# Latent attention: row maxima of two key pieces together, with a 32-row rotary part from the query's high part alone

## The chip, the cores and the metric

The kernel runs on one core of a Trainium2 chip. The metric is the device time of one execution in microseconds (us), as the median of several runs. The core's engines are called as the profile calls them: PE (matrix unit; its weight loads are listed apart as PEld), DVE (vector), ACT (scalar, activations), POOL (GpSimd) and SP (the queue from which most transfers are issued). PE multiplies a stationary operand (the weights, up to 128x128) with a moving one of up to 512 columns, and writes into PSUM, which has eight banks of 512 float32 columns on 128 partitions. A matmul whose operands use only 64 of the 128 partitions is put on half of PE's rows (a tile of 64 rows); in this kernel's timeline two such matmuls on different halves run side by side. The change uses tiles of 32 rows as well.

## The reference

Two layers over 1024 latent tokens and 256 context tokens of width 1024: the first is windowed attention, the second is multi-head latent attention (16 heads, 64 plain and 32 rotary dimensions for a query and a key, 64 for a value), then a final RMS norm. The change is in the second layer's attention:

```python
def attend(qn, qr, kn, kr, v):
    s = (jnp.einsum("bqhd,bkhd->bhqk", qn, kn)
         + jnp.einsum("bqhd,bkd->bhqk", qr, kr)).astype(F32) * scale
    p = jax.nn.softmax(s, axis=-1).astype(v.dtype)
    return jnp.einsum("bhqk,bkhd->bqhd", p, v)
```

The rotary keys `kr` are the same for all heads. All inputs are float32.

## The kernel before

Products are made in a fast float32 format of PE. Where more precision is wanted, an operand is split into a high and a low part of that format, and the product is made of several matmuls (high x high, low x high, high x low). `split` makes the two parts of an operand: a cast on ACT and a subtraction on DVE (or POOL).

The attention of the second layer is made in 16 units (`class UnitB`). A unit is a pair of heads and half of the latent queries (512). The two heads `e` of a pair lie on the two halves of the partitions (`HALF`), so that their matmuls run as a pair on PE's two 64-row halves. The 1280 keys are taken in ten chunks of 128 for the scores and three pieces of 512, 512 and 256 (`KEYB`) for the maxima. The operands of a unit are:

- `kt`, the plain part of the keys of the pair, high and low, and `KR`, the rotary part, repeated four times over the partitions, so that each 32 rows hold all of it; `KR[:, 0]` is the high part;
- `q`, the queries, in four slots: 0 and 1 are the plain part (high, low); in slot 2 the first 32 rows of each half hold the rotary high part and the other 32 rows the rotary low part; in slot 3 the first 32 rows of each half hold the rotary high part, and rows 32 to 35 the negated maxima, which `shift` writes there. `prep` loads them from DRAM, with one load for slots 0 and 1 and two per head for the rotary ones.

For each unit:

- **Maxima** (`top`, L1754 its matmuls, L1760 and L1762 its reductions). With queries as stationary operand and keys as moving one, a piece is two matmuls per head: slot 0 with the high plain keys (64 rows), and slot 2 with `KR[:, 0]` (64 rows: the query's high and low rotary parts with the key's high part). They add up in one bank per head. DVE then takes the maximum over the bank's columns. There are four blocks `b` of 128 queries and three pieces `i` of keys; the 256-wide pieces are taken two blocks together in one bank. `PIECES` is the list of ten, one for each score chunk. The banks come from a ring of three (`topb`: 0, 1, 2), which the fills share.
- **Shift** (`turn`, `shift`). The maxima of a unit are joined, turned by PE and written as four more rows of the query operand, so that the scores come out with the maximum subtracted.
- **Scores** (`score`, L1788). For each chunk `c` five matmuls per head, terms 0 to 4; the last has 36 rows, 32 rotary ones and four of the shift. `bank(c)` alternates between two pairs of banks (3 and 4, 5 and 6). When the fifth term is issued, `exp(c)` (L1798) follows on ACT, one activation over both banks, and POOL adds it up for the sum of the softmax (L1802, L1804).
- **PV** (`PV`, L1811). The exponentials of each chunk with the values, in 128x64 tiles, added up in bank 7 over all ten chunks. `fin` copies bank 7 out on ACT (L1815) and loads the gate. `fin2` makes the sum over partitions (L1822), `inv` the reciprocal, `gate` the product with the gate on POOL.
- **Fill**. Between units, `make_K` (each other unit) or `make_V` (each fourth unit) makes the keys of the next pair or the values of the next four heads with 128-row matmuls (L285 to L287).

Everything from the units on is issued in program order; each engine takes its own instructions in that order. The loop over units interleaves them by hand: the maxima of the next unit `nu` are made between the scores of the present unit `u`. In each chunk PE takes score terms 0 to 2, then one piece of the next unit's maxima, then score terms 3 and 4. After the ten chunks, `prep` of the unit after the next is issued, PV(0), the sums of the previous unit, PV(1) to PV(4), the turn of the next unit's maxima, PV(5) to PV(9), then a fill where there is one, then `fin`. The maxima of unit 0 are made ahead of the loop, with banks that are named there. So the loop makes the maxima of 15 units.

```python
u.score(c, 0, CUT)
if nu:
    nu.top(PIECES[c])
if c == 0 and ui > 1:
    units[ui - 2].gate()
u.score(c, CUT, 5)
```

Of the kernel before, what the change touches and what calls it, by code (L numbers as in the profile page):

```python
# [16 lines left out]
AX = mybir.AxisListType  # L17
# [18 lines left out]
class Ring:  # L36
# [6 lines left out]
    def next(self):  # L43
        b = self.bufs[self.i % len(self.bufs)]
        self.i += 1
        return b


def shp(ap, *dims):
    n = 1  # L50
    for d in dims:
        n *= d
    ap = ap[:, 0:n]
    if len(dims) == 1:
        return ap
    names = "abcdefg"[: len(dims)]
    kw = {c: d for c, d in zip(names[1:], dims[1:])}
    return ap.rearrange("p (" + " ".join(names) + ") -> p " + " ".join(names), **kw)
# [159 lines left out]
def kernel(ctx: ExitStack, tc: tile.TileContext, t, out, dbg=None):  # L218
    plan = Plan()
    nc = Recorder(tc.nc, plan)  # L220
# [4 lines left out]
    PB = ppool.tile([128, 8, 512], F32, name="PB")  # L225
# [16 lines left out]
    load = nc.sync.dma_start  # L242
    load2 = nc.scalar.dma_start

    def r_at(kb, *dims):
        n = int(np.prod(dims))
        return shp(R[:, int(kb * KB) : int(kb * KB) + n], *dims)
# [298 lines left out]
    for p in (1, 3):  # L546
        two = R[:, 16 * p * KB : 16 * (p + 2) * KB]
# [105 lines left out]
    class UnitA:  # L653
# [23 lines left out]
        def prep(self):  # L677
            ti, g = self.ti, self.g
            self.gt = shp(gr.next(), 2, 128)
            load(out=self.gt, in_=g0_d[2 * g : 2 * g + 2, :, ti * 128 : ti * 128 + 128].rearrange("c p n -> p c n"))  # L680
            self.mx, self.nm, self.den, self.esk = sm_ring(), sm_ring(), sm_ring(), sm_ring()
# [195 lines left out]
    def turn(p, b, bank):  # L877
        tbank[p, b] = ps = shp(PB[:, bank, :], 2, 256)
        for kk in range(2):
            for j in range(2):  # L880
                c0 = (2 * b + kk) * 128
                nc.tensor.transpose(ps[:, kk, j * 128 : j * 128 + 128], xn[p][0][:, j, c0 : c0 + 128], ident)
# [129 lines left out]
    for i in range(3, NG):  # L1012
        p, q = groups[i]
# [47 lines left out]
    for bi, gp, c in order:  # L1061
# [20 lines left out]
        r = proj_t(bi, gp, c)  # L1082
# [43 lines left out]
    for ui, u in enumerate(units):  # L1126
# [9 lines left out]
        nu = units[ui + 1] if ui + 1 < len(units) else None  # L1136
# [4 lines left out]
        for ci in range(u.m):  # L1141
# [3 lines left out]
            if ci == 0:  # L1145
# [6 lines left out]
                if ui in (24, 27, 30, 33, 36):  # L1152
                    i = ui // 3 - 8
# [3 lines left out]
            i = u.g * u.m + ci - 1  # L1157
# [338 lines left out]
    for k in range(8):  # L1496
        w0_cut1(k, nc.vector if k % 2 else nc.gpsimd)
        if k % 2:
            b = k // 2
# [4 lines left out]
    def turn_two():  # L1504
        if todo:
            p, b = todo.pop(0)
            for i in range(2):
                turn1(p, b + i, turns)
            return p, b
# [14 lines left out]
    two = turn_two()  # L1524
# [10 lines left out]
    two = turn_two()  # L1535
    for ti in range(NT):
# [6 lines left out]
        now, two = two, turn_two()  # L1543
# [11 lines left out]
        if 4 <= ti < 8:  # L1555
            i = ti - 4
# [32 lines left out]
    for n, i in enumerate((2, 3, 4, 5, 0, 1)):  # L1589
        ps = product(a12r[i], B21)  # L1590
        x = outs.next()
# [65 lines left out]
    KR = r_at(20, 2, TOK)  # L1657
# [4 lines left out]
    otr = Ring(F, [0, 2], 512)  # L1662
    glr = Ring(R, [30, 112, 150], 512)
    KEYB = ((0, 512), (512, 512), (1024, 256))
    PIECES = [[(0, 0)], [(0, 1)], [(1, 0)], [(1, 1)], [(0, 2), (1, 2)]]
    CUT = 3
    PIECES += [[(b + 2, i) for b, i in p] for p in PIECES]
    flat = krF.rearrange("p a b -> p (a b)")
    mxr = [flat[:, 128 * i : 128 * i + 128] for i in range(2)]
    mxpr = [shp(flat[:, 256 + 24 * i : 280 + 24 * i], 2, 4, 3) for i in range(2)]  # L1670
    ones = sm(64)
    nc.vector.memset(ones, 1.0)
    fillb = Banks(0, 1, 2)
    topb = Banks(0, 1, 2)
    psd = PB[:, 5, :]
    HALF = [slice(64 * e, 64 * e + 64) for e in range(2)]

# [16 lines left out]
    def make_V(quad):  # L1694
        for tp in range(NP):
            ps = fillb()
            for j in range(2):
                ti = 2 * tp + j
                for k in range(2):
                    mm3(  # L1700
                        ps[:, j * 256 : j * 256 + 256],
                        [ckvT[:, s, k, ti * 128 : ti * 128 + 128] for s in range(2)],
                        [ukV[:, s, k, quad * 256 : quad * 256 + 256] for s in range(2)],
                        k == 0, k == 1,
                    )
            nc.scalar.copy(Vq[:, 2 * tp : 2 * tp + 2], shp(ps, 2, 4, 64))
            yield

    def make_K(pair):
        kt = kTb[pair % 2]  # L1710
        for n0, n in KEYB:
            ps = fillb()
            for k in range(2):
                mm3(
                    ps[:, 0:n],
                    [ukK[:, s, k, pair * 128 : pair * 128 + 128] for s in range(2)],
                    [ckvT[:, s, k, n0 : n0 + n] for s in range(2)],
                    k == 0, k == 1,
                )
            split(kt[:, 0, n0 : n0 + n], kt[:, 1, n0 : n0 + n], ps[:, 0:n])  # L1720
            yield
# [3 lines left out]
    class UnitB:  # L1725
# [11 lines left out]
        def prep(self):  # L1737
            q = self.q.bitcast(F32)
            load(out=q[:, 0:2], in_=qn_d[self.pair, :, :, self.ts])
            for e in range(2):  # L1740
                r = 32 * ((2 * self.pair + e) % 4)
                src = qr_d[self.pair // 2, r : r + 32, :, self.ts]
                load(out=q[64 * e : 64 * e + 32, 2:4], in_=src[:, 0:1].to_broadcast([32, 2, 512]))
                load(out=q[64 * e + 32 : 64 * e + 64, 2], in_=src[:, 1])

        def top(self, piece, banks=None):

            banks = banks or (topb(), topb())
            n = KEYB[piece[0][1]][1]
            for j, (b, i) in enumerate(piece):  # L1750
                n0, o, bs = KEYB[i][0], 256 * j, slice(b * 128, b * 128 + 128)
                for s, k in ((0, self.kt), (2, KR)):
                    for bank, r in zip(banks, HALF):
                        nc.tensor.matmul(  # L1754
                            bank[:, o : o + n], self.q[r, s, bs], k[r, 0, n0 : n0 + n], start=s == 0, stop=s == 2
                        )
            b, i = piece[0]
            for e, bank in enumerate(banks):
                if len(piece) == 1:
                    nc.vector.reduce_max(self.mxp[:, e, b : b + 1, i], bank[:, 0:n], AX.X)  # L1760
                else:
                    nc.vector.reduce_max(self.mxp[:, e, b : b + 2, i], shp(bank, 2, 256), AX.X)  # L1762

        def turn(self, bank):
            nc.vector.reduce_max(shp(self.mx, 2, 64)[:, :, 32:36], self.mxp, AX.X, negate=True)
# [96 lines left out]
    def fetch_out(ti):  # L1862
        o = shp(ogl.next(), 8, 128)
        load(out=o.bitcast(F32), in_=og_d[:, :, ti * 128 : ti * 128 + 128].rearrange("c p n -> p c n"))
        x = xr1.next().bitcast(F32)
        load(out=x, in_=x1_d[256 + ti * 128 : 384 + ti * 128, :])
        return o, x

    def cut_out(f):
        o, x = f  # L1870
        og = shp(ogr1.next(), 2, 8, 128)
        for h in range(2):
            hs = slice(4 * h, 4 * h + 4)
            split(og[:, 0, hs], og[:, 1, hs], o[:, hs].bitcast(F32))
        return og, x
# [87 lines left out]
    fillb = Banks(6, 7)  # L1963
# [11 lines left out]
    fillb = Banks(0, 1, 2)  # L1975
    nc.scalar.activation(const[:, 1:2], const[:, 1:2], AF.Exp)
    wo_fill = wo_pieces()
    for ui, u in enumerate(units):
        pu = units[ui - 1] if ui else None
        nu = units[ui + 1] if ui + 1 < NU else None  # L1980
        nnu = units[ui + 2] if ui + 2 < NU else None
        for c in range(NT):
            if c == 5 and nu is None:
                pu.fin2(PB[:, 2, :])
                u.PV(0, 5)
                pu.inv(0)
                pu.gate(0, 256)
                first = fetch_out(0)
                pu.inv(1)
                pu.gate(256, 512)  # L1990
                got = fetch_out(1)
            u.score(c, 0, CUT)
            if nu:
                nu.top(PIECES[c])
            if c == 0 and ui > 1:
                units[ui - 2].gate()
            u.score(c, CUT, 5)
            if 0 < ui < 12 and c == 2 or ui == 6 and c == 7 or ui in (12, 13) and c in (2, 7):
                next(wo_fill, None)
            if nu is None and c == 0:  # L2000
                load(out=gx1, in_=gate_d[1, 0, :].partition_broadcast(128))
                load(out=fg, in_=t["final_g"].partition_broadcast(128))
        if nnu:
            nnu.prep()
        if nu is None:
            u.PV(5, NT)
        else:
            b = u.bank(NT - 2)
            u.PV(0, 1)
            u.exp(NT - 1)  # L2010
            if pu:
                pu.fin2(PB[:, b, :])
            u.PV(1, 5)
            nu.turn(PB[:, b + 1, :])
            nu.shift()
            if pu:
                pu.inv(0)
                pu.inv(1)
            u.PV(5, NT)
        if nu:  # L2020
            fillb.i = topb.i
            fill = make_K(u.pair + 1) if u.half == 0 and u.pair < 7 else iter(())
            if ui % 4 == 3:
                fill = make_V(ui // 4 + 1)
            for _ in fill:
                pass
        else:
            ready = cut_out(first)
        u.fin()
    u.fin2(psd)  # L2030
    for j in range(2):
        u.inv(j)
# [78 lines left out]
```

## Time and profile before

| what | before |
|---|---|
| median of 3 runs | 1489.13 us (1488.36 to 1490.11) |
| the profiled execution | 1488.73 us, its span 1486.9 us |
| mean granted clock of PE | 0.997 |
| busy: PE, DVE, ACT, POOL | 98%, 72%, 49%, 55% of the span |
| the 16 units of latent attention | from about 927 to 1393 us of the span |
| one scoring stage (ten chunks of one unit; units 0 to 14) | 16.5 to 16.8 us |
| one PV stage | 9.8 us, then a fill of 3.65 or 7.4 us, or none |

A line of a group reads: line of the kernel, engine, operation, what is written from what, shapes (partitions x elements), count, then busy time and the mean of one, then idle time ahead of it with what ended most of it. A timeline's row gives the start and length of a run of equal instructions in us, the engine, the line, the operation, the shape of the first one, and the count; in brackets stands the idle time ahead of it and what ended it. Matmuls overlap, so that the sum of their lengths is more than their busy time; the distance from start to start tells what one costs.

### The profile page before, as it was taken

What the parts mean: (1) busy time and instruction counts of PE and PEld (TensorE: products, weight loads), DVE (VectorE), ACT (ScalarE), POOL (GpSimd) and SP (SyncE); (2) the same over time, 40 slices, a digit from 0 to 9 for tenths busy, and PEclk for the clock granted to TensorE, in tenths of its full rate; (3) what the DMA queues carried; (4) which work ended last, traced back from release to release, by engine and by line L of the source; (5) the groups of instructions that cost most, each with busy time, mean ns of one, the idle gap of its engine ahead of it and who ended that gap; (6) DMA issues with size and microseconds to landing.
All of it is one profiled execution on the core that took longest, in us unless ns stands there. A gap on an engine that the chain in (4) does not pass through costs nothing.

```text
span 1486.9 us, 25072 instructions
## 1 busy us (share of the span) xinstructions
PE 1462.6 (98%) x9036; PEld 1188.3 (80%) x9036; DVE 1064.1 (72%) x2029; ACT 733.5 (49%) x1397; POOL 810.4 (55%) x735
## 2 busy tenths in 40 slices
PE   6999999999999999999999999999999999999998
PEld 4888888888888888888888888766777767876687
DVE  3787789738778888878988777666576466566764
ACT  4421222359888878876554432443454344444321
POOL 2563366346454444456300240798788788789371
PEclk9999999999999999999999999999999999999999
DMA  9545644673343333336444566011122212120442
GB/s 336 170 171 170 212 150 169 208 223 114 121 144 119 98 101 98 100 100 229 119 120 119 169 234 207 21 41 53 47 63 70 62 47 61 54 68 28 151 152 86
DMA packets 146964, 186.01 MB, mean 125 GB/s; under 512 B 12812, under 2 KB 100492, under 8 KB 146840
## 3 DMA queue, kind: packets, MB, share of 16 engines
q1 hardware_dynamic: 141864, 177.75, 37.7%
q10 hardware_dynamic: 4976, 6.66, 1.3%
q8 instruction: 71, 1.16, 0.3%
q14 instruction: 53, 0.43, 0.1%
HBM read 134.02 MB, written 46.15 MB: 121 GB/s over the span
## 4 chain that ended last, share of the span: by engine, by line
PE 49%; DVE 2%; issue 1%; DMA 0%; POOL 0%; ACT 0%; POOLq 0%; DVEq 0%; ACTq 0%
PE PB L1788 13%; PE PB L1811 9%; PE PB L285 7%; PE PB L287 7%; PE PB L286 7%; PE PB L1754 5%; PE PB L1822 1%; DVE arena_r L281 1%; DMA arena_r<-arena_f 0%; PE PB L1768 0%; DVE arena_f L1327 0%; DVE krF L1760 0%; DVE arena_f L1236 0%; DVE arena_f L1329 0%; DVE arena_f L1328 0%
## 5 line engine op out<-in xcount | busy, mean ns | idle before, releaser
L285 PE MATMUL PB<-arena_r 128*128 128x512 f32 (+2 forms) x1200 | 439.4, 366 | 1.3 <-DVE arena_f L1236 1.3
L286 PE MATMUL PB<-arena_r 128*128 128x512 f32 (+2 forms) x1200 | 433.7, 361 | 0.1
L287 PE MATMUL PB<-arena_r 128*128 128x512 f32 (+2 forms) x1200 | 433.3, 361 | 0.0
L1804 POOL TENSOR_TENSOR arena_f<-arena_f 128x1024 f32<-128x1024 f32 x120 | 285.9, 2382 | 8.2
L285 PEld LDWEIGHTS PB<-arena_r 128*128 128x128 f32 x1200 | 226.3, 189 | 45.7 <-issue 9.0
L287 PEld LDWEIGHTS PB<-arena_r 128*128 128x128 f32 x1200 | 226.3, 189 | 33.7
L286 PEld LDWEIGHTS PB<-arena_r 128*128 128x128 f32 x1200 | 226.5, 189 | 32.2 <-POOL arena_r L281 0.8
L1788 PE MATMUL PB<-arena_r 64*128 64x512 f32 (+1 forms) x1600 | 229.6, 395 | 0.0
L1798 ACT ACTIVATE arena_f<-PB 128x1024 f32<-128x1024 f32 x160 | 164.5, 1028 | 112.0 <-PE PB L1788 84.0
L1760 DVE TENSOR_REDUCE krF<-PB 128x1 f32<-128x512 f32 (+1 forms) x264 | 167.0, 678 | 65.7 <-PE PB L1754 65.6
L1788 PEld LDWEIGHTS PB<-arena_r 64*128 64x128 f32 (+1 forms) x1600 | 179.4, 185 | 14.7 <-issue 5.2
L704 DVE CUSTOM_DVE_ANT_0 arena_f<-PB,arena_f,small 128x256 f32<-128x256 f32 (+1 forms) x288 | 148.1, 525 | 51.9 <-PE PB L698 33.3
L280 ACT CAST arena_r<-PB 128x512 fp32r<-128x512 f32 (+2 forms) x207 | 115.3, 564 | 113.2 <-PE PB L287 73.3
L281 DVE TENSOR_TENSOR arena_r<-PB,arena_r 128x512 fp32r<-128x512 f32 (+2 forms) x207 | 134.3, 661 | 34.7 <-ACT arena_r L280 34.1
L1811 PE MATMUL PB<-arena_f 128*64 128x512 f32 x640 | 145.9, 595 | 0.0
L281 POOL TENSOR_TENSOR arena_r<-arena_f,arena_r 128x512 fp32r<-128x512 f32 (+1 forms) x64 | 87.9, 1388 | 102.9 <-ACT arena_r L280 89.4
L710 ACT ACTIVATE arena_f<-arena_f,small 128x640 f32<-128x640 f32 (+2 forms) x160 | 119.1, 745 | 15.8 <-DVE small L704 13.6
L280 ACT CAST arena_r<-arena_f 128x512 fp32r<-128x512 f32 (+1 forms) x142 | 82.2, 611 | 87.3 <-PE PB L287 28.3
L507 DVE SCALAR_TENSOR_TENSOR arena_f<-arena_f,small 128x512 f32<-128x512 f32 x98 | 114.0, 1208 | 10.9 <-DMA arena_f<-ada_w 10.6
L737 PE MATMUL PB<-arena_r 128*128 128x512 f32 x336 | 118.6, 429 | 0.0
L1754 PE MATMUL PB<-arena_r 64*128 64x512 f32 (+1 forms) x768 | 114.2, 355 | 0.1
L727 PE MATMUL PB<-ident,arena_f 128*128 128x128 f32 x672 | 108.6, 272 | 0.1
(215 smaller groups left out, 2087.2 us busy)
## 6 DMA issues: line engine op xcount, KB each, us to landing
arena_f<-ada_w SPq DMA_DIRECT2D x96, 256.0 KB, 4.1
arena_r<-q_d SPq DMA_DIRECT2D x160, 128.0 KB, 2.8
arena_f<-a_w_in SPq DMA_DIRECT2D x40, 256.0 KB, 3.9
arena_f<-b_w_in SPq DMA_DIRECT2D x36, 256.0 KB, 2.9
arena_f<-x SPq DMA_DIRECT2D x16, 512.0 KB, 5.8
q_d<-arena_f SPq DMA_DIRECT2D x16, 512.0 KB, 3.0
arena_r<-qn_d SPq DMA_DIRECT2D x16, 512.0 KB, 5.0
g_d<-arena_f ACTq DMA_DIRECT2D x20, 256.0 KB, 3.7
```

Of the source, the lines that this page charges most:

```text
L280: nc.scalar.copy(hi, src)
L281: (lo_eng or nc.vector).tensor_sub(lo, src, hi.bitcast(F32))
L285: nc.tensor.matmul(o, ah, bh, start=first, stop=False)
L286: nc.tensor.matmul(o, al, bh, start=False, stop=False)
L287: nc.tensor.matmul(o, ah, bl, start=False, stop=last)
L704: nc.vector.tensor_tensor_reduce(o, S, mk, -A_SCALE, prev, ALU.add, ALU.min, mx)
L1754: nc.tensor.matmul(bank[:, o : o + n], self.q[r, s, bs], k[r, 0, n0 : n0 + n], start=s == 0, stop=s == 2)
L1760: nc.vector.reduce_max(self.mxp[:, e, b : b + 1, i], bank[:, 0:n], AX.X)
L1788: nc.tensor.matmul(PB[:, b + e, :], k[r, s, cs], q[r, sq], start=i == 0, stop=i == 4)
L1798: nc.scalar.activation(E, PB[:, b : b + 2, :], AF.Exp)
L1804: eng.tensor_add(acc, acc, E)
L1811: nc.tensor.matmul(PB[r, 7, :], Vq[:, c, h, :], E[:, e], start=c == 0, stop=c == NT - 1)
```

## The change

The maxima are made two pieces at a time by a new function, `top2`, in every second chunk (five doubles per unit). The plain part is as before: for each piece and head one matmul of 64 rows. The rotary part takes the query's high part alone, on 32 rows: slot 3 now holds the high part a second time on rows 32 to 63 of each half, by one more load per head in `prep`, so that the four matmuls of two pieces and two heads use four different 32-row tiles. Each writes its own bank, of 0, 1, 2 and 7. All plain matmuls of a double come first, then all rotary ones, then the four reductions in the order of the banks. The low part of the rotary query no longer enters the maxima; since the maximum is only subtracted ahead of the exponential, and the same shift enters the sum, the result needs it only roughly. `fin`, which reads bank 7, moves ahead of the fill, and the fill's banks start again at 0. The ring `topb` goes; unit 0 still uses `top`.

```diff
-    PIECES = [[(0, 0)], [(0, 1)], [(1, 0)], [(1, 1)], [(0, 2), (1, 2)]]
+    PIECES = [[[(b, 0)], [(b, 1)]] for b in range(4)]
+    PIECES.insert(2, [[(0, 2), (1, 2)], [(2, 2), (3, 2)]])
     CUT = 3
-    PIECES += [[(b + 2, i) for b, i in p] for p in PIECES]
...
     fillb = Banks(0, 1, 2)
-    topb = Banks(0, 1, 2)
...
                 load(out=q[64 * e + 32 : 64 * e + 64, 2], in_=src[:, 1])
+                load(out=q[64 * e + 32 : 64 * e + 64, 3], in_=src[:, 0])
...
+        def top2(self, two):
+
+            banks = [PB[:, i, :] for i in (0, 1, 2, 7)]
+            n = KEYB[two[0][0][1]][1]
+            for s in (0, 3):
+                for j in range(len(two[0])):
+                    for x, piece in enumerate(two):
+                        b, i = piece[j]
+                        n0, bs, cs = KEYB[i][0], slice(b * 128, b * 128 + 128), slice(256 * j, 256 * j + n)
+                        for e, r in enumerate(HALF):
+                            if s:
+                                r = slice(r.start + 32 * x, r.start + 32 * x + 32)
+                            k = (KR if s else self.kt)[r, 0, n0 : n0 + n]
+                            nc.tensor.matmul(
+                                banks[2 * x + e][:, cs], self.q[r, s, bs], k,
+                                start=s == j == 0, stop=s == 3 and j == len(piece) - 1,
+                            )
+            for x, piece in enumerate(two):
+                b, i = piece[0]
+                for e in range(2):
+                    bank = banks[2 * x + e]
+                    if len(piece) == 1:
+                        nc.vector.reduce_max(self.mxp[:, e, b : b + 1, i], bank[:, 0:n], AX.X)
+                    else:
+                        nc.vector.reduce_max(self.mxp[:, e, b : b + 2, i], shp(bank, 2, 256), AX.X)
...
             u.score(c, 0, CUT)
-            if nu:
-                nu.top(PIECES[c])
+            if nu and c % 2 == 0:
+                nu.top2(PIECES[c // 2])
...
         if nu:
-            fillb.i = topb.i
+            u.fin()
+            fillb.i = 0
             fill = make_K(u.pair + 1) if u.half == 0 and u.pair < 7 else iter(())
...
         else:
             ready = cut_out(first)
-        u.fin()
+            u.fin()
```

More of the change, by code (lines that the diff above doesn't have):

```diff
@@ L1744, in prep, with top @@
                 load(out=q[64 * e + 32 : 64 * e + 64, 2], in_=src[:, 1])
-        def top(self, piece, banks=None):
-            banks = banks or (topb(), topb())
+                load(out=q[64 * e + 32 : 64 * e + 64, 3], in_=src[:, 0])
+        def top(self, piece, banks):
             n = KEYB[piece[0][1]][1]
```

## The prediction

> **What bounds the kernel now.** I read the page first (busy time, the chain that ended last, the costliest groups), then the stages of one attention unit by windows, then PE's timeline inside such a unit, and last what PE waited for.
>
> ```profile
> span 1486.9 us, 25072 instructions
> ...
> PE 1462.6 (98%) x9036; PEld 1188.3 (80%) x9036; DVE 1064.1 (72%) x2029; ACT 733.5 (49%) x1397; POOL 810.4 (55%) x735
> ...
> PE 49%; DVE 2%; issue 1%; DMA 0%; POOL 0%; ACT 0%; POOLq 0%; DVEq 0%; ACTq 0%
> ...
> L1798 ACT ACTIVATE arena_f<-PB 128x1024 f32<-128x1024 f32 x160 | 164.5, 1028 | 112.0 <-PE PB L1788 84.0
> L1760 DVE TENSOR_REDUCE krF<-PB 128x1 f32<-128x512 f32 (+1 forms) x264 | 167.0, 678 | 65.7 <-PE PB L1754 65.6
> ...
> L1754 PE MATMUL PB<-arena_r 64*128 64x512 f32 (+1 forms) x768 | 114.2, 355 | 0.1
> ```
>
> PE is busy nearly all the span and leads the chain; the other engines wait for it. So time is won only by taking work from PE without giving PE something to wait for. L1754, the maxima, is 768 matmuls: 48 for each of 16 units, of which the change touches 15 (unit 0's are made elsewhere). The windows over one unit without a fill:
>
> ```profile
> 1196.94:1213.56 16.62, 16.62 (x149) 15.28 (x148) 13.00 (x21) 10.62 (x12) 12.16 (x7) 1.00 0.10 33
> 1213.56:1223.37 9.81, 9.81 (x50) 3.29 (x48) 5.13 (x7) 1.50 (x2) 9.50 (x5) 1.00 0.46 121
> ```
>
> The first row is the scoring stage of a unit (ten key chunks, with the next unit's maxima between them), the second its PV stage; the columns are length, then busy time of PE, weight loads, DVE, ACT and POOL. The change acts in the first, 16.62 us, and at its border with the second.
>
> **The stream that goes.** PE's timeline in a scoring stage, and DVE's row for the second piece of it:
>
> ```profile
> 1171.32 1.43 PE L1788 MATMUL PB<-arena_r 64*128 64x512 f32 x10
> 1172.49 0.72 PE L1754 MATMUL PB<-arena_r 64*128 64x512 f32 x4
> 1172.94 1.42 PE L1788 MATMUL PB<-arena_r 64*128 64x512 f32 x10
> 1174.11 0.72 PE L1754 MATMUL PB<-arena_r 64*128 64x256 f32 x8
> 1174.58 0.40 PE L1788 MATMUL PB<-arena_r 64*128 64x512 f32 x1
> ```
> ```profile
> 1173.14 1.29 DVE L1760 TENSOR_REDUCE krF<-PB 128x1 f32<-128x512 f32 x2 [0.33 <-PE PB L1754]
> ```
>
> Matmuls on the two 64-row halves run side by side, so I count pairs. From 1171.32 to 1172.49 are five score pairs: 0.23 us each. From 1172.49 to 1172.94 are two pairs of a piece: 0.23 again. Four 256-wide pairs take 1174.58 - 1174.11 = 0.47, so 0.117 each. A unit's maxima are 16 wide and 8 narrow passes; after the change they are 12 and 6 if four 32-row matmuls run in one pass. That saves 4 x 0.23 + 2 x 0.117 = 1.15 us a unit, 17.3 us in 15 units. The number of instructions stays.
>
> **The switches that come.** Each double goes from 64-row to 32-row tiles and back: ten switches a unit. No row has a 32-row tile, so the nearest are other changes of tile shape:
>
> ```profile
> 1192.75 0.60 PE L1811 MATMUL PB<-arena_f 128*64 128x512 f32 x2
> 1193.28 0.50 PE L285 MATMUL PB<-arena_r 128*128 128x512 f32 x1
> 1193.62 0.40 PE L286 MATMUL PB<-arena_r 128*128 128x512 f32 x1
> 1193.86 0.39 PE L287 MATMUL PB<-arena_r 128*128 128x512 f32 x1
> ```
> ```profile
> 1196.73 0.28 PE L287 MATMUL PB<-arena_r 128*128 128x256 f32 x1
> 1196.94 0.97 PE L1788 MATMUL PB<-arena_r 64*128 64x512 f32 x6
> 1197.74 0.46 PE L1754 MATMUL PB<-arena_r 64*128 64x512 f32 x2
> ```
> ```profile
> 1375.67 0.39 PE L1788 MATMUL PB<-arena_r 36*128 36x512 f32 x2
> 1375.99 1.08 PE L1822 MATMUL PB<-arena_f,small 128*64 128x512 f32 x4
> 1376.90 0.60 PE L1811 MATMUL PB<-arena_f 128*64 128x512 f32 x2
> ```
>
> From 128 to 64 rows: 1196.73 to 1197.74 is 1.01 for one narrow matmul (0.12) and three pairs (0.69), so 0.20 over. From 1192.75 to 1193.62 is 0.87 where a PV pair (0.43 in a stream) and a matmul of 0.23 make 0.66: 0.21 over. Into 128x64 tiles it is least: 0.32 instead of 0.23 before, and 0.91 instead of 0.86 behind, 0.14 in all. The 0.20 has two parts: the array runs empty (about 0.09), then the first matmul lasts 0.50 instead of 0.39 since its weights could not be loaded ahead (about 0.10). I take 0.20 (the row-to-row case is the nearest): 10 x 0.20 = +2.0 us a unit. Bounds: nothing, if 32 rows are no new shape; 0.30 on average, if four first loads take turns where two now start together (two more of 0.10, on one of each two switches).
>
> The Trainium skill, "TensorEngine Tiling (Array Packing)", Key Properties, says that a change of tiling mode drains the array while another tile of the same mode does not, and lists 64 and 32 rows as different modes; that speaks against this change and no run shows it yet. By the drain the sum below stands; were 32 rows only another tile, it would be the free-switch rival's. "TensorE: Matmul & The Clock Gate", Measured speedup vs the span model, gives 3.07 times for four 32-row tiles; by that figure a double's last pass takes 4/3.07 = 1.3 passes, about 5 us more in all (an estimate from that page).
>
> **The wait on exp.** Scores use two pairs of banks in turn, so chunk c+2 needs exp(c) done. Today every chunk also holds a piece of maxima; after the change odd chunks hold none, and PE arrives sooner.
>
> ```profile
> 1376.16 1.02 ACT L1798 ACTIVATE arena_f<-PB 128x1024 f32<-128x1024 f32 x1
> ```
> ```profile
> 1207.39 1.03 ACT L1798 ACTIVATE arena_f<-PB 128x1024 f32<-128x1024 f32 x1 [0.89 <-PE PB L1788]
> ```
> ```profile
> 1208.47 0.30 PEld L1788 LDWEIGHTS PB<-arena_r 64*128 64x128 f32 x4 [0.25 <-ACT arena_f L1798]
> ```
> ```profile
> 1207.90 1.54 PE L1788 MATMUL PB<-arena_r 64*128 64x512 f32 x10
> 1209.28 0.62 PE L1754 MATMUL PB<-arena_r 64*128 64x512 f32 x4
> ```
>
> The last score pair of a chunk starts at 1375.67, its exp at 1376.16: 0.49. The exp lasts 1.03, and PE follows its end by 0.05 (1207.39 + 1.03 = 1208.42, weights at 1208.47). So chunk c+2 may start 1.57 after the last pair of chunk c. With an odd chunk of five pairs between, PE is there after six pairs, 1.38: 0.19 early, plus 0.10 for weights not loaded ahead. That is 0.29, before chunks 2, 4, 6 and 8: +1.16 us a unit. The trace of before has one such wait, and there five pairs took 1.38 (1207.90 to 1209.28) instead of 1.17: 0.21, the same order; behind it queue all of PE's scores, so nothing hides it. Bounds 0.1 to 0.4 each.
>
> **The wait on bank 7.** A double's four maxima are reduced in the order of its banks, bank 7 last, and PV accumulates into bank 7. From PE's second top pair (1172.49 + 0.23) to DVE's start at 1173.14 is 0.43. Two reductions of 0.69 take 1.29, so they follow at 0.60, and four take 2.49. With 0.10 for the weights of the 32-row matmuls and 0.05 to release PE, bank 7 is free 0.10 + 0.43 + 2.49 + 0.05 = 3.07 after the last 32-row matmuls are issued. PE has two score pairs, chunk 9's five and the entry to PV left: first pair at 0.42, second at 0.75, seventh at 1.90, PV at 2.22. PV waits 0.85 a unit, and with PE everything behind it: PV(1..9), the turn of the maxima, the next fill. Today the last reductions end under PV, which uses another bank. Between doubles PE comes to bank 7 at about 3.3, later than 3.07: no wait there. Bounds: 0.5 to 1.1.
>
> **Edits at no cost.**
>
> ```profile
> 1214.96 0.42 SPq L1744 DMA_DIRECT2D arena_r<-qr_d  x1
> ```
> ```profile
> DMA to landing us min/median/max: 3.2/4.9/6.4
> ```
> ```profile
> 1223.49 0.59 ACT L1815 COPY arena_f<-PB 128x512 f32<-128x512 f32 x1 [7.24 <-PE PB L1811]
> ```
> ```profile
> 1218.98 4.46 PE L1811 MATMUL PB<-arena_f 128*64 128x512 f32 x20
> 1223.37 0.97 PE L1788 MATMUL PB<-arena_r 64*128 64x512 f32 x6
> 1224.18 0.64 PE L1754 MATMUL PB<-arena_r 64*128 64x512 f32 x4
> ```
>
> Two more loads a unit on SP's queue take 0.84; they come ahead of fin's load (SP is idle behind it), and the last lands near 1214.96 + 0.42 + 0.84 + 4.9 = 1221.1, 3 us before the maxima at 1224.18 in a unit without fill, the shortest case. PV covers them. The bank-7 copy of fin (0.59), moved ahead of the fill on ACT, ends at 1224.08; the first double wants bank 7 one pair after 1224.18. In units with a fill it has 3.6 us more. Without that cover it would cost up to 0.59 a unit. The fill's banks restart at 0; its third eviction may hold the first double 0.1 us in 7 units: under 1 us.
>
> **The sum.** Per unit -1.15 + 2.0 + 1.16 + 0.85 = +2.86. The pairs of before add up to 66 x 0.23 + 8 x 0.117 + 0.2 at the ends = 16.3, and the stage takes 16.62: some 0.3 is lost where the halves run out of step. A drain puts them in step, so I give back half: 2.86 - 0.15 = 2.71, times 15 = 40.7 us. The profiled execution took 1488.7 (its span of 1486.9 and 1.8 around it; the runs' median is 1489.1): 1488.7 + 40.7 = **1529.4 us**.
>
> **The rivals.**
> - *Free switch.* If 32-row tiles join the 64-row stream without a drain, the 2.0 goes. The exp wait stays 1.16, PV's wait becomes (0.43 + 2.49 + 0.05) - (7 x 0.23 + 0.32) = 1.04: +1.05 a unit, 1488.7 + 15.8 = 1504.5. For it: 36-row matmuls (1375.67) sit among 64-row ones at no price. Against: they are in tiles of the same shape.
> - *Not four at once.* If the 32-row matmuls run two by two, the 1.15 is not saved: 1529.4 + 17.3 = 1546.7. Against: two halves overlap fully today. That is also the case in which the change doesn't do what it says.
> - *Faster.* PE never catches up with ACT and DVE: the switch is free and the banks come back in time, so only the stream counts, 1488.7 - 17.3 = 1471.4. Its place is the odd chunk and the entry to PV; it decides where those waits stay under 1.15 a unit, and the rows give 1.16 + 1.04 = 2.2. It needs exp and reductions that start far sooner behind PE than 0.49 and 0.43. Waits of half the size give no change.
>
> **How the numbers follow.** Forecast (drain and waits, 1515 to 1540) 0.65; free switch 0.15; not four at once 0.07; about no change 0.05; faster 0.08. The least and greatest prices of the switch, with the waits' bounds, put the range at 1500 to 1541, which leaves out the last three. A measurement of this kernel tells some 0.2% (3 us) from no change. Faster 0.08, same 0.05, slower 0.87.
>
> **What would show it.** Right: scoring stages of about 19.3 us; gaps of PE's weight loads before each 32-row group and behind it, and a first matmul of 0.50; five waits a unit of L1788 or L1811 on ACT and on DVE's reductions; PV stages still 9.8. Wrong: 32-row rows that start 0.23 behind a 64-row pair (free switch); pairs of 32-row rows 0.23 apart (not four at once); a PV entry without a wait on DVE (my order of reductions); scoring stages under 16.6.

## The result, and the profile after

The changed kernel takes 1530.1 us (median of five runs, 1529.2 to 1530.6) against 1489.1 us for the kernel before in the same series: 1.0275 times, 95% interval 1.026 to 1.029. It is 41 us slower; 1529.4 us was forecast, with a range of 1500 to 1541.

The page of the changed kernel, with the lines that answer to those of before:

```profile
span 1528.0 us, 25062 instructions
...
PE 1491.4 (98%) x9036; PEld 1132.8 (74%) x9036; DVE 1054.4 (69%) x2029; ACT 733.3 (48%) x1397; POOL 808.9 (53%) x735
...
PE 48%; DVE 4%; issue 1%; DMA 0%; ACT 0%; POOL 0%; POOLq 0%; DVEq 0%; ACTq 0%
...
L1836 PE MATMUL PB<-arena_f 128*64 128x512 f32 x640 | 145.9, 595 | 11.2 <-DVE krF L1785 11.2
```

The lines have moved: scores are L1813 now, `top2`'s matmuls L1776 and its reductions L1785 and L1787, exp L1823, PV L1836. PE still leads the chain and has as many instructions as before; DVE's share of the chain is 4% where it was 2%, and PV's matmuls now wait 11.2 us for a reduction of the maxima, which they did not do at all before.

Windows over one unit, scoring stage and then PV stage (columns as before):

```profile
1188.85:1208.21 19.36, 18.48 (x150) 11.90 (x149) 12.45 (x21) 10.24 (x11) 13.92 (x7) 1.00 0.00 1
1208.21:1218.02 9.81, 9.81 (x49) 3.29 (x49) 4.21 (x5) 1.50 (x2) 9.57 (x5) 1.00 0.53 135
```

The scoring stage takes 19.36 us where the one shown of before took 16.62; the PV stage takes 9.81 in both. Over the 15 units that the change touches, the scoring stages sum to 290.4 us, and to 249.0 before: 41.4 us, which is the whole difference of the spans (41.1). So the loss lies where the change is, and what was lost or won elsewhere is within 0.3 us.

Inside the stage, PE's timeline around the end of an odd chunk and the double behind it, and PE's weight loads and ACT in the same stretch:

```profile
1191.74 1.88 PE L1813 MATMUL PB<-arena_r 64*128 64x512 f32 x12
1193.45 1.06 PE L1776 MATMUL PB<-arena_r 64*128 64x512 f32 x8
1194.44 0.97 PE L1813 MATMUL PB<-arena_r 64*128 64x512 f32 x6
```
```profile
1192.63 0.54 PEld L1813 LDWEIGHTS PB<-arena_r 64*128 64x128 f32 x6 [0.48 <-ACT arena_f L1823]
...
1194.00 0.19 PEld L1776 LDWEIGHTS PB<-arena_r 32*128 32x128 f32 x4 [0.36 <-issue]
1194.44 0.30 PEld L1813 LDWEIGHTS PB<-arena_r 64*128 64x128 f32 x4 [0.25 <-issue]
```
```profile
1191.56 2.16 ACT L1823 ACTIVATE arena_f<-PB 128x1024 f32<-128x1024 f32 x2 [2.01 <-PE PB L1813]
```

- The wait on exp: the first of the two exps ends at 1191.56 + 1.03 = 1192.59, and the next scores' weights are loaded at 1192.63. The six score pairs from 1191.74 take 1.71 instead of 6 x 0.23 = 1.38: 0.33 lost, where 0.29 was worked out. The trace has both parts of it: the pair that waited starts 0.21 late, and the next one 0.11 later than in a stream, since the waiting pair's weights were not loaded ahead.
- The switches: no weights are loaded ahead into the 32-row group (0.36 of idle time, ended by nothing that the profile shows) nor out of it (0.25). From 1193.45 to 1194.44 are two pairs and one pass, 0.69 in a stream, and 0.99 here. The six matmuls that follow last 0.97 together, where three pairs in a stream last 2 x 0.23 + 0.39 = 0.85. That is 0.30 + 0.12 = 0.42 for two switches, 0.21 each; 0.20 was forecast.
- The four 32-row matmuls do run at once: their four weight loads of 0.18 us each lie in one row of 0.19 us. Grouped by shape over the units (the window of this view has 59 of the 60 wide doubles):

```profile
L1776 PE MATMUL PB<-arena_r 32*128 32x512 f32 x236 | 29.9, 496 | 0.0
```

These 236 matmuls are 59 groups of four; their joint busy time of 29.9 us is 0.51 a group, no more than the length of a single one (0.496).

The border to PV, on DVE and on PE:

```profile
1205.67 2.48 DVE L1785 TENSOR_REDUCE krF<-PB 128x1 f32<-128x512 f32 x4 [1.20 <-PE PB L1776]
```
```profile
1205.57 1.89 PE L1813 MATMUL PB<-arena_r 64*128 64x512 f32 x14
1208.21 0.65 PE L1836 MATMUL PB<-arena_f 128*64 128x512 f32 x2 [0.75 <-DVE krF L1785]
```

The four reductions of the last double end at 1205.67 + 2.48 = 1208.15, and PV starts 0.06 later, after 0.75 us in which PE did nothing. On the mean of 14 units PV starts 3.06 us behind the issue of the last 32-row matmuls.

### The profile page after: what moved, and what is told of

Same layout as the page of the kernel before. It is cut to its first block, busy times and chain, and to the rows that moved or that the text cites. A ratio compares the mean times of both kernels' runs of the same rounds, so it can differ in the third digit from the quotient of the medians.

```text
span 1528.0 us, 25062 instructions
## 1 busy us (share of the span) xinstructions
PE 1491.4 (98%) x9036; PEld 1132.8 (74%) x9036; DVE 1054.4 (69%) x2029; ACT 733.3 (48%) x1397; POOL 808.9 (53%) x735
## 3 DMA queue, kind: packets, MB, share of 16 engines
q8 instruction: 71, 1.16, 0.3%
## 4 chain that ended last, share of the span: by engine, by line
PE 48%; DVE 4%; issue 1%; DMA 0%; ACT 0%; POOL 0%; POOLq 0%; DVEq 0%; ACTq 0%
PE PB L1813 13%; PE PB L1836 9%; PE PB L285 7%; PE PB L286 6%; PE PB L287 6%; PE PB L1776 5%; DVE krF L1785 2%; PE PB L1847 1%; DVE arena_r L281 1%; PE PB L1753 0%; PE PB L1793 0%; DMA arena_r<-arena_f 0%; DVE krF L1759 0%; DVE arena_f L1236 0%; DVE arena_f L1329 0%
## 5 line engine op out<-in xcount | busy, mean ns | idle before, releaser
L1823 ACT ACTIVATE arena_f<-PB 128x1024 f32<-128x1024 f32 x160 | 164.4, 1028 | 159.4 <-PE PB L1813 122.7
L1813 PE MATMUL PB<-arena_r 64*128 64x512 f32 (+1 forms) x1600 | 226.3, 411 | 1.4
L1785 DVE TENSOR_REDUCE krF<-PB 128x1 f32<-128x512 f32 x240 | 149.1, 684 | 93.1 <-PE PB L1776 93.1
L1813 PEld LDWEIGHTS PB<-arena_r 64*128 64x128 f32 (+1 forms) x1600 | 138.8, 185 | 72.3 <-ACT arena_f L1823 27.3
L1836 PE MATMUL PB<-arena_f 128*64 128x512 f32 x640 | 145.9, 595 | 11.2 <-DVE krF L1785 11.2
L1836 PEld LDWEIGHTS PB<-arena_f 128*64 128x64 f32 x640 | 44.0, 137 | 91.6 <-issue 73.5
```

The lines of the kernel that those rows point to most:

```text
L1813: nc.tensor.matmul(PB[:, b + e, :], k[r, s, cs], q[r, sq], start=i == 0, stop=i == 4)
L1823: nc.scalar.activation(E, PB[:, b : b + 2, :], AF.Exp)
L1836: nc.tensor.matmul(PB[r, 7, :], Vq[:, c, h, :], E[:, e], start=c == 0, stop=c == NT - 1)
```

## The experiments

The theory: three costs, each in its own place, that add up: switches of tile height less the saved passes (+0.85 us a unit), the wait on exp behind odd chunks (+1.16), PV's wait on bank 7 (+0.85). The rivals: that one cause (the switch) makes nearly all of it, or that the two waits share a cause, so that one grows when the other goes. The first four runs take the costs apart.

**Bank 7 first.** The only edit is the order of a double's banks, and so of the reductions:

```diff
-            banks = [PB[:, i, :] for i in (0, 1, 2, 7)]
+            banks = [PB[:, i, :] for i in (7, 0, 1, 2)]
```

> The changed kernel with the banks of a double in the order 7, 0, 1, 2, so that bank 7 is reduced first. My theory: PV then finds bank 7 free some 1.3 us after the last 32-row matmuls, before it comes there (2.2 us), so PV's wait of 0.75 to 0.82 us a unit goes and nothing takes its place: 1530.1 - 15 x 0.82 = 1518 us (1516 to 1520), scoring stages of 18.6 us. Rival (the order of the reductions does not matter, PV waits for all four, or the turn of the maxima takes over the wait): 1530 us. Second rival (bank 7 is now wanted one pair sooner in chunk 0, while ACT still copies it): 1518 plus up to 0.3 us a unit, 1522 us.

Measured: 1518.2 us, 1.0194 times the kernel before (1.0179 to 1.0209). This is the theory's number. PV waits for no reduction any more and starts 2.25 us behind the last 32-row matmuls (3.06 in the changed kernel), and the wait on exp stays what it was (27.0 us in all, 27.3 in the changed kernel). Scoring stages are 18.5 to 18.7 us in nearly all units. So the order of the four reductions cost 12 us.

**64 rows.** The rotary part as before the change, in the same doubles:

```diff
-            for s in (0, 3):
+            for s in (0, 2):
...
-                            if s:
-                                r = slice(r.start + 32 * x, r.start + 32 * x + 32)
...
```

> The changed kernel with the rotary part of a double on 64 rows again (slot 2, high and low part, as before the change): no change of tile height, no saved pass; doubles, bank 7 and the order stay. My theory: against the kernel before, the stream is the same, the wait on exp stays at 0.32 us four times a unit (1.28) and PV's wait on bank 7 grows to 1.0: 1489 + 15 x 2.2 = 1522 us (1517 to 1525), scoring stages of 18.7 to 18.9 us. Rival (nearly all of the loss is the switch between tile heights, the waits only fill time that is lost anyway): 1489 to 1495 us. Second rival (a switch costs twice what I take, the waits half): 1505 us.

Measured: 1516.7 us, 1.0185 (1.017 to 1.020), just under the range that was expected, far from both rivals. The kernel does the matmuls of the kernel before, in another order and partly into other banks, and loses 27.7 us. What PE's units waited for:

```profile
PEld PB L1811 <- ACT arena_f L1821: 27.1, 60, 0.5
...
PE PB L1834 <- DVE krF L1783: 10.9, 15, 0.7
```

The 60 waits on exp are there (four in each of 15 units), and PV's wait is 10.9 / 15 = 0.73, not the 1.0 that was expected: with 64-row rotary pairs the banks of the first piece are complete one pair (0.23) ahead of those of the second, so that DVE starts sooner. In the trace DVE's first reduction starts 0.19 us behind the last matmul of the maxima, and 0.52 behind the last 32-row one in the changed kernel, where the switch adds some 0.10 to it. The expected term left this pair out.

**64 rows and bank 7 first.** Both edits together.

> The kernel of the run with 64 rows, with bank 7 reduced first as well: of the three costs only the wait on exp is left. My theory: 1489 + 15 x 1.28 = 1508 us (1504 to 1510), scoring stages of 17.6 to 17.9 us, four waits a unit of the scores' weight loads on exp. Rival (the two waits share their cause, and with one gone the other grows): 1520 us. Second rival (the wait on exp is idle time that PE loses anyway in the stream before): 1489 us.

Measured: 1505.4 us, 1.0106 (1.009 to 1.0123). As the theory has it; the wait on exp does not grow when the other goes:

```profile
PEld PB L1811 <- ACT arena_f L1821: 27.4, 60, 0.7
```

**Singles on 32 rows.** The kernel before, with nothing but a switch there and back in each piece; the low part of the rotary query is left out of the maxima, as the change does:

```diff
                     for bank, r in zip(banks, HALF):
+                        r = slice(r.start, r.start + 32) if s and self.i else r
```

> The kernel before with one edit: in units 1 to 15 the rotary part of each single piece takes the first 32 rows of slot 2 alone (the query's high part), so that every piece goes from 64-row to 32-row tiles and back; the low part of the rotary query is left out of these maxima. No doubles, no bank 7, no saved pass. Eight pieces with two switches and two with four make 24 a unit. My theory: 24 x 0.20 = 4.8 us a unit, less 0.2 to 0.3 for halves that fall in step: 1489 + 15 x 4.55 = 1557 us (1550 to 1561), scoring stages of 21.2 us, no wait on exp or on the reductions. Rival (32 rows are only another tile of the same shape, no drain): 1489 us. Second rival (the price seen at the quads comes from four first weight loads, not from the switch): half the price, 1520 to 1525 us.

Measured: 1558.5 us, 1.0466 (1.045 to 1.0481): 69.5 us, 4.63 a unit, 0.193 for each of 24 switches (less whatever the halves win by falling in step, which they do here). Here only two weight loads come first behind a switch, not four, and the price is nearly the same, so it is the switch and not the number of loads. The trace says it closer: from the last plain pair through the 32-row matmuls to the next scores it takes 0.754 us on the mean here, and 0.775 with four of them in the changed kernel. The windows of one scoring stage:

```profile
1100.82:1122.11 21.29, 21.29 (x150) 13.23 (x149) 13.18 (x21) 10.61 (x12) 15.41 (x7) 1.00 0.06 15
```

PE counts as busy in all of its 21.29 us, though 4.7 of them are new and do no work: the switch is hidden within the lengths of the matmuls, and only weight loads that wait for no other engine show it.

**The double split over two chunks**, with bank 7 first: an attempt to keep the 32-row groups and lose the two waits.

```diff
...
-            if nu and c % 2 == 0:
-                nu.top2(PIECES[c // 2])
+            if nu and c % 2:
+                nu.top2(PIECES[c // 2], 1)
...
             u.score(c, CUT, 5)
+            if nu and c % 2 == 0:
+                nu.top2(PIECES[c // 2], 0)
```

Part 0, behind the even chunk's scores, is the plain matmuls of the first piece; part 1, in the odd chunk, is all the rest, all 32-row matmuls among it.

> The changed kernel with each double spread over two chunks: the plain matmuls of its first piece behind the even chunk's scores, those of the second and the four 32-row ones in the odd chunk, and bank 7 first among the banks. My theory: an even chunk then holds a pair more, PE comes back to the scores' banks 1.61 us after a chunk's last pair where exp needs 1.57, so the wait on exp goes; PV finds bank 7 at 1.27 and comes at 1.07, a wait of 0.2 at most. What is left is the switches less the saved passes: -1.15 + 2.0 + 0.2 a unit, less 0.15 for halves in step: 1489 + 15 x 0.9 = 1502 us (1499 to 1505), scoring stages of 17.5 us. Rival (the wait on exp is not a matter of where the maxima stand, the chip holds PE back behind the 32-row groups): 1515 to 1518 us, as with bank 7 first alone.

Measured: 1507.2 us, 1.0128 (1.0114 to 1.0142), neither number. The waits shrank but did not go:

```profile
PEld PB L1817 <- ACT arena_f L1827: 9.6, 44, 0.5
...
PEld PB L1840 <- DVE krF L1789: 8.1, 15, 0.6
```

PV's wait was expected: it starts 0.18 us later than in the run with bank 7 first and no wait, and 0.2 at most was worked out. The wait on exp was not: the margin of 0.04 us that was worked out for it (1.61 against 1.57) was too fine, and 44 of 60 places still wait, 0.2 each, of which some is paid. The rival (PE is held back behind the 32-row groups) falls: two thirds of the wait's total (27 to 9.6 us) went with the place of one pair, and the runs on 64 rows have the whole wait without any such group. But the forecast was 5 us too low.

**The same split on 64 rows**: no switch, no saved pass. Each part is now a whole piece, plain and rotary, so that the even chunk gets one pair more than in the split run.

> The kernel of the split run with the rotary part on 64 rows (each piece's own matmuls in its chunk's place, high and low part): no switch, no saved pass, no wait. My theory: the three costs named are all there are, so this is the kernel before again, 1489 us (1487 to 1492), scoring stages of 16.5 to 16.7 us, and the split run less this one is what the 32-row groups cost net, 15 x 0.85 = 13 us. Rival (bank 7 for the maxima, the moved copy of fin or the added loads cost something of their own): 1493 us or more.

Measured: 1486.0 us against 1488.3 before, 0.9984 (0.9975 to 0.9993): 2.3 us faster than the kernel before, little, but outside the interval, and just under the range that was expected. It keeps bank 7 for the maxima, the moved copy and the added loads, so these cost no more together than the run wins elsewhere; PV's weights wait for a reduction still (5.3 us in 15 places), but PV starts no later for it. One of its scoring stages (14 of the 15 take 16.37 to 16.49, the first takes 17.06):

```profile
1046.60:1062.98 16.38, 16.38 (x149) 13.30 (x148) 11.43 (x19) 10.34 (x11) 11.45 (x6) 1.00 0.01 2
```

Another expectation failed: the split run less this one was to be what the 32-row groups cost, 13 us, and it is 1507.2 - 1486.0 = 21.2. The trace of the split run has the better part of the rest in the waits that stayed (PV's 0.18 a unit, and some 0.2 for exp), so this difference does not measure the groups alone.

**The loads alone**, in the kernel before:

```diff
+                load(out=q[64 * e + 32 : 64 * e + 64, 3], in_=src[:, 0])
```

> The kernel before with the two added loads a unit alone (the second copy of the rotary high part, which nothing reads). My theory: PV covers them: 1489 us, within 1.5. Rival (SP's queue or the transfers delay the next unit's maxima): about 0.4 us a unit for each load that comes late, 1495 us.

Measured: 1488.2 us against 1488.3, 1.0003 (0.9994 to 1.0012). The loads cost nothing, as the theory has it.

**Why is the split on 64 rows faster than the kernel before?** Its two halves start 3 to 4 ns apart all through a stage, in 14 of 15 stages; in the kernel before, one falls behind by up to 100 ns and more. Two edits of the kernel before were to tell the banks from the place. First, fixed pairs of banks, with `fin` moved as in the change:

```diff
-                nu.top(PIECES[c])
+                nu.top(PIECES[c], [PB[:, i, :] for i in ((7, 0), (1, 2))[c % 2]])
...
```

> The kernel before with single 64-row pieces in each chunk as there, but with fixed pairs of banks (7 and 0 for even pieces, 1 and 2 for odd ones) in place of the ring of three, and fin ahead of the fill. In the split run on 64 rows the two halves of a pair start 3 to 4 ns apart all through a scoring stage, in the kernel before up to 100 ns and more, and the stage takes 16.4 instead of 16.6 us. Theory A (two pieces that share a bank of the ring let one half fall behind): the halves keep in step here too, stages of 16.4 us, 1486 us. Theory B (it is the place of the even piece behind its chunk's scores): no change here, 16.6 us, 1489 us.

And the place alone, with the ring of three banks:

```diff
-            if nu:
+            if nu and c % 2:
                 nu.top(PIECES[c])
...
             u.score(c, CUT, 5)
+            if nu and c % 2 == 0:
+                nu.top(PIECES[c])
```

> The kernel before with one edit: the single piece of each even chunk stands behind that chunk's five score terms instead of between the third and the fourth; the ring of three banks and everything else stay. Theory A (the ring of banks): no change, stages of 16.6 us, 1489 us. Theory B (the place): halves in step, stages of 16.4 us, 1486 us.

Measured: 1487.9 against 1489.1 (0.9995, 0.9986 to 1.0004) for the banks, 1502.0 (1.0088, 1.0074 to 1.0102) for the place. Neither theory holds. With fixed banks the halves stay in step in 11 of 15 stages, yet such a stage takes 16.53 us, not 16.38: being in step is worth 0.07 at the most. (This run also shows that bank 7 for the maxima and the moved copy cost nothing that can be measured.) The place alone costs 13 us, by a wait that neither theory had:

```profile
PEld PB L1754 <- DVE krF L1760: 15.9, 58, 0.4
```

With three banks for pieces of two, the odd chunk's piece, which now follows the even one after three pairs, wants a bank whose reduction is not done. The remaining 0.15 us a stage between the fixed banks and the split run on 64 rows stays open. It is no wait: most of it is that score pairs follow each other at 234 ns on the mean in the one and at 237 in the other, 39 times a stage.

## Why the prediction was right, point by point

Each run is first taken against the kernel before in its own series: +41.0 us for the change, +29.2 with bank 7 first, +27.7 on 64 rows, +16.4 with both edits and -2.3 for the split on 64 rows. Differences of these, divided by 15 units, give the costs:

| term | forecast, us a unit | measured, us a unit | from |
|---|---|---|---|
| switches less saved passes | -1.15 + 2.0 = 0.85 | (41.0 - 27.7) / 15 = 0.89; (29.2 - 16.4) / 15 = 0.85 | with and without 32 rows |
| wait on exp | 1.16 | 16.4 / 15 = 1.09; (16.4 + 2.3) / 15 = 1.25 | both edits, against the kernel before; against the split on 64 rows |
| PV's wait on bank 7 | 0.85 | (41.0 - 29.2) / 15 = 0.79; (27.7 - 16.4) / 15 = 0.75 | bank order |

The first and the third term come out nearly the same with the other cost present and without it, so they add. The second is what is left, from a run that differs in the order of the work as well. That the three make up the 41.0 us again is so by construction; the timeline of the changed kernel is a check of its own. There, switches less saved passes come to some 0.93 us a unit, the waits on exp to 4 x 0.29 = 1.17, and PV's start is 3.06 - 2.25 = 0.81 late. Together that is 2.91 us over the stages of 16.38 of the split on 64 rows, which has none of the three; the changed kernel's stages take 19.38 on the mean, 3.00 more.

- *The bound* was read rightly: PE leads, so a saved pass counts in full, and so does each wait of PE.
- *The saved stream* is real: four 32-row matmuls take one pass. That the change does not do what it says, or that the groups run two by two, is refuted by the group of 59 x 0.51 us.
- *The switch* at 0.20, taken from changes between other shapes, was 0.193 in the run that has it alone and 0.21 in the timeline. The free-switch rival falls with that run. The Trainium skill's rule ("TensorEngine Tiling (Array Packing)", Key Properties) that a change of tiling mode drains the array agrees with this case; the same page lists 64 and 32 rows as different configurations (Available Configurations). The price is the runs'. The factor of 3.07 for four 32-row tiles that the Trainium skill gives ("TensorE: Matmul & The Clock Gate", Measured speedup vs the span model) does not show here: by the prediction's estimate from it a wide double's last pass would take 0.07 us more than one pass, and four 32-row matmuls take 0.775 - 0.754 = 0.02 us more than two between the same switches. The measurement decides.
- *The wait on exp* was forecast at 0.29 each (PE 0.19 early, 0.10 for weights not loaded ahead); the one shown is 0.33, and the mean over 14 units is 0.29 (0.19 and 0.11), both parts as worked out. The split run shows that it hangs on how much stands between two uses of a pair of banks.
- *The wait on bank 7* was forecast at 0.85 and measured at 0.75 to 0.79. The steps of DVE were right: PV starts 3.06 us behind the last 32-row matmuls, and 3.07 was worked out. PE without the wait would come at 2.25, not 2.22.
- *The half credit* of 0.15 for halves in step hit the total: the terms before it make 2.86 a unit, and the stages grew by 2.76. Its condition came true, since the changed kernel's halves start 3 to 4 ns apart in most pairs, but its reason is not confirmed: halves in step were worth 0.07 at the most in the run with fixed banks, and the split on 64 rows gains 0.15 more for which no cause is shown. That the credit fits so well is luck, and that the total fits to 1 us is in part luck too, since small errors of the terms cancel.
- *The range* does not follow from the bounds that were given: all least or all greatest, with the half credit, they make some 1483 to 1555 us, not 1500 to 1541. The 1530.1 lies well inside both, but the working does not show where the narrower range comes from.
- *The faster rival* needed both waits to vanish and the switch to be free. With 32 rows even the best order that was tried, the split one, takes 1507 us.

So the 32-row groups are a net loss by themselves: a double saves one pass of 0.23 (two narrow ones in the narrow double) and pays two switches of 0.20, with either order of the banks. The order of the work cost about twice as much again (1.09 to 1.25 for exp, and 0.77).

## What to carry to other kernels

Price a change of tile shape on PE as time, some 0.2 us each way here, even if PE shows no idle time: look at whether weights are loaded ahead across it. Where work is moved from every step to every second step, look at the step that is left short: what it had been covering (here exp's 1.03 us and the 0.49 us ahead of it) is then on the path. And a bank that the next stage needs goes first in the order of the engine that frees it: that alone was worth 12 us.

## What was not expected of the hardware

The two halves of PE can run apart by over 100 ns for a whole stage and lose almost nothing by it (stages of 16.6 us, against 16.53 with halves in step and fixed banks). A change of tile height leaves no idle time in PE's row: PE counted as busy for all of a stage that held 4.7 us of switches.
